# Turned signs in a seven-product step: the first weight sum becomes u0 + g0, added in place by an accumulating DMA, and the first feed-forward uses four such steps a pass instead of three

## The chip, the cores and the metric

The kernel runs on one core of a Trainium2 chip. The metric is the time of one execution on the device in microseconds, as the median of several runs. Before the change three runs gave 2245.61, 2246.25 and 2247.01 us.

## What is computed

One decoder layer on 256 tokens (T) of width 2048 (D), all in float32: a SwiGLU feed-forward (width 5632), a mixer of windowed attention and a recurrent part, an attention into a fixed memory, a second feed-forward, and a last norm. Only the two feed-forwards matter here:

```python
def swiglu(h, w_gate, w_up, w_down):
    return (jax.nn.silu(h @ w_gate) * (h @ w_up)) @ w_down

x = x + 0.5 * swiglu(rms_norm(x, ffn1_norm[l]), ffn1_w_gate[l], ffn1_w_up[l], ffn1_w_down[l])
# mixer, cross-attention
x = x + 0.5 * swiglu(rms_norm(x, ffn2_norm[l]), ffn2_w_gate[l], ffn2_w_up[l], ffn2_w_down[l])
```

## The kernel before, in words

**Two parts of each number.** A float32 value is kept as a high part `hi`, rounded to the type that TensorE multiplies fast, and a rest `lo`. ScalarE (ACT in the profile) makes `hi` by a cast (`split_unit`, L400), VectorE (DVE) makes `lo` by a subtraction (L401). One product of a 128-token block with a 128x512 block of weights is three matmuls of 512 columns, hi by hi, hi by lo and lo by hi (`times`, L474 to L479).

**Steps.** The feed-forward goes through column blocks of 512: `feed_forward` (L718) has a loop over groups of column blocks, and for each block j after the first one call of `gate_and_up`, which is one *pass* (ten a feed-forward). A pass multiplies the 256 tokens by the j-th 512 columns of the gate matrix and of the up matrix, over all 2048 rows. Its unit of work is a *step*, called q in the code, of 256 rows: two 128x512 blocks of gate, g0 and g1, and two of up, u0 and u1. A pass has eight steps, q = 0 to 7. `down` does the same for two column blocks of the down matrix. The order of the products is written in `product_pair` (L537).

**Seven products for eight.** With two blocks of tokens, two of rows and two matrices a step is a 2x2 by 2x2 block product: 8 products, 24 matmuls. In some steps a scheme of the Strassen kind takes 7 products (21 matmuls) and sums on both sides instead. The sums on the weight side are four 128x512 float32 operations on DVE (`divide`, L429 to L432); they fill two tiles t0 and t1, which are then split into `thi` and `tlo` like any weight (`two_parts`, L408 and L409). Of the tiles loaded, g0, g1 and u1 are still multiplied too, u0 is not. Which steps do so is listed by hand: `SEVEN = (0, 2, 4)` for the passes of the first feed-forward, `SEVEN_2 = (0, 2, 3, 4)` for those of the second, `SEVEN_DOWN` for the down matrix. Step 3 of the second feed-forward is *staged*: its sums are made during the mixer (`stage`, L371), written to a DRAM tensor `sums`, and read back by `load_sums` (L361). The sums on the token side are made once a feed-forward, in `combinations` (L489).

**Buffers and their order.** The SP queue loads the weights (`load`, L337): one DMA brings 1 MB, four blocks of one matrix, so that a gate tile and an up tile together feed two steps, (0,1), (2,3), (4,5) or (6,7). There are four such tiles, two pairs: the loads for the pair of steps after next start when DVE has read the last of a tile. `hi` and `lo` have three buffers each and are taken in turn, gate then up: the `hi` of a step's gate waits until TensorE has done with the up weights of two steps before, the `hi` of its up for the gate weights of the step before. `thi` and `tlo` have one buffer for each of t0 and t1. `next_item` (L436) divides one step ahead of TensorE. The program is written as one stream of instructions; a scheduler puts them in a fixed order on each engine before the run, and each engine then executes its own in that order, waiting on semaphores.

In the prediction, "behind" an instruction means after it in that fixed order.

Of the kernel before, what the change touches and what calls it, by code (L numbers as in the profile page):

```python
# [15 lines left out]
P = 128  # L16
# [120 lines left out]
def decoder_layer(ctx: ExitStack, tc: tile.TileContext, a: dict, out: bass.AP):  # L137
# [175 lines left out]
    for entry in weight_plan(a):  # L313
        if entry is None:
            ends.append(len(units))
            continue
        plan.append(entry)
        w, k0, nk, c0, n = entry
        if not isinstance(w, tuple):
            for k in range(k0, k0 + nk, KU):  # L320
                items.append(((len(units),), False))
                units.append((w, k, c0, n))
            continue
        for k in range(k0, k0 + nk, 2 * KU):
            u = len(units)
            units += [(v, k + i, c, 512) for v, c in zip(w, c0) for i in (0, KU)]
            for i in range(2):
                q = (k - k0) // KU + i
                if n == SEVEN_2 and q in STAGED:
# [3 lines left out]
    first_unused = {items[i][0][1] for i in staged}  # L333
    sums_d = dram.tile([len(staged), P, 4, 512], F32, name="sums")
    at = {"item": 0, "product": 0, "pool": None}

    def load(u, pieces=None):  # L337

        if u >= len(units) or u in raws:
            return  # L340
        w, k, c0, n = units[u]
        wide = at["pool"] is not None and (u < ends[0] or u >= ends[1] + LOADED)
        m = 2 if wide else 1
        if wide:
            raw = at["pool"].tile([P, m * KU, n], F32, tag="raw2", name="raw2", bufs=4)
# [4 lines left out]
        if u in first_unused:  # L350
            second = u + 1 in first_unused
            pieces = [(slice(1, 2), nc.sync)] + [(slice(2 + second, 4), nc.sync)]
            if not second:
                pieces = ((slice(1, 4), nc.sync),)
        elif u + 1 in first_unused and wide:
            pieces = ((slice(0, 2), nc.sync), (slice(3, 4), nc.sync))
        for i, queue in pieces or ((slice(0, m * KU), nc.sync),):
            rows = slice((k + i.start) * P, (k + i.stop) * P)
            queue.dma_start(raw[:, i], w[rows, c0 : c0 + n].rearrange("(a p) n -> p a n", p=P))

    def load_sums(i):  # L361

        if i not in staged or i in summed:
            return
        summed[i] = [
            wp.tile([P, KU, 512], F32, tag="raw", name="raw", bufs=4) for _ in range(2)
        ]
        for e, t in enumerate(summed[i]):
            nc.sync.dma_start(t[:], sums_d[staged[i], :, KU * e : KU * e + KU, :])

    def stage(t4, i, n):  # L371


        while at["item"] < STAGE_AT[n]:
            yield
        t = t4("su", (P, KU, 512)), t4("sg", (P, KU, 512))
        for e, v in zip(t, items[i][0][::-1]):
            w, k, c0, _ = units[v]
            rows = slice(k * P, (k + KU) * P)
            nc.sync.dma_start(e[:], w[rows, c0 : c0 + 512].rearrange("(a p) n -> p a n", p=P))  # L380
        yield from idle(4)
        u0, u1, g0, g1 = (e[:, c] for e in t for c in range(KU))
        with tc.issue_after(at["lo"].ins):
            dve.tensor_tensor(g0, u0, g0, ALU.subtract)
            dve.tensor_tensor(u0, u1, u0, ALU.subtract)
        yield
        with tc.issue_after(at["lo"].ins):
            dve.tensor_tensor(u1, u1, g0, ALU.subtract)
            dve.tensor_tensor(g1, g1, u1, ALU.subtract)
        yield from idle(8)  # L390
        for c, e in enumerate(t):
            nc.sync.dma_start(sums_d[n, :, KU * c : KU * c + KU, :], e[:])
# [8 lines left out]
            at["lo"] = dve.tensor_tensor(lo[:, s], raw[:, s], f32(hi[:, s]), ALU.subtract)  # L401
        return hi, lo

    def two_parts(v, e):
        sp = at["pool"]
        hi = sp.tile([P, KU, 512], F32R, tag="thi" + e, name="thi")
        lo = sp.tile([P, KU, 512], F32R, tag="tlo" + e, name="tlo")
        act.copy(hi[:], v[:])  # L408
        dve.tensor_tensor(lo[:], v[:], f32(hi[:]), ALU.subtract)  # L409
        return hi, lo  # L410

    def divide(i):


        if i >= len(items) or i in parts:
            return
        which, seven = items[i]
        if len(which) == 1:
            parts[i] = split_unit(*which)
            return  # L420
        g, u = which
        if not seven:
            parts[i] = split_unit(g), split_unit(u)
            return
        t = summed.get(i)
        if t is None:
            rg, ru = raws[g], raws[u]
            t = [wp.tile([P, KU, 512], F32, tag="raw", name="raw", bufs=4) for _ in range(2)]
            dve.tensor_tensor(t[1][:, 0], ru[:, 0], rg[:, 0], ALU.subtract)  # L429
            dve.tensor_tensor(t[0][:, 0], ru[:, 1], ru[:, 0], ALU.subtract)  # L430
            dve.tensor_tensor(t[0][:, 1], ru[:, 1], t[1][:, 0], ALU.subtract)  # L431
            dve.tensor_tensor(t[1][:, 1], rg[:, 1], t[0][:, 1], ALU.subtract)  # L432
# [56 lines left out]
    def combinations(sp, x: Act, seven, name, ready=lambda: True, early=True, n=0):  # L489
# [8 lines left out]
        def work():  # L498
# [3 lines left out]
            for q in pairs:  # L502
# [9 lines left out]
                    )  # L512
                if q in seven:
                    n = 4
                    dve.tensor_tensor(f[:, 0], v[:, 0, 1], v[:, 1, 1], ALU.add)
                    dve.tensor_tensor(f[:, 1], f[:, 0], v[:, 0, 0], ALU.subtract)
                    dve.tensor_tensor(f[:, 2], v[:, 0, 0], v[:, 0, 1], ALU.subtract)
# [19 lines left out]
    def product_pair(x: Act, c, w, first, middle, out):  # L537
# [67 lines left out]
    def gate_and_up(sp, x: Act, c, r, w):  # L605
# [5 lines left out]
            act.copy(hb[:, 0], b["p1"][:])  # L611

        def middle(b):
            dve.tensor_tensor(u2[:], b["p6"][:], hb[:, 0], ALU.add)
# [5 lines left out]
        def out(b, to):  # L620
            t = int(to in ("p4", "p5"))
            if to in ("p2", "p4"):
                dve.tensor_tensor(hb[:, t], b[to][:], u3[:] if t else hb[:, 0], ALU.add)
# [9 lines left out]
    def down(sp, h: Act, c, w, xs):  # L633

        u2, u3 = sums_of(sp)

        def half(x_, v):
            dve.scalar_tensor_tensor(x_, v, 0.5, x_, ALU.mult, ALU.add)

        def first(b):  # L640
            act.copy(u3[:], b["p1"][:])
# [1 line left out]
            half(xs[1][1], b["q"][:])  # L643

        def middle(b):
            dve.tensor_tensor(u2[:], b["p6"][:], u3[:], ALU.add)
            dve.tensor_tensor(u3[:], b["p7"][:], u2[:], ALU.add)
            dve.tensor_tensor(u2[:], b["p5"][:], u2[:], ALU.add)
            half(xs[1][0], u3[:])
            half(xs[1][1], u3[:])  # L650
            half(xs[0][1], u2[:])

# [65 lines left out]
    def feed_forward(sp, x, norm: Norm, wg, wu, wd, done, begin_last=lambda: None, last=False):  # L718
        if last:
            for tag, shape, dt, bufs in (  # L720
                ("hhi", [P, 16, T], F32R, 1), ("hlo", [P, 16, T], F32R, 1),
                ("hb", [P, 2, 512], F32, 2), ("thia", [P, KU, 512], F32R, 1),
                ("tloa", [P, KU, 512], F32R, 1), ("thib", [P, KU, 512], F32R, 1),
                ("tlob", [P, KU, 512], F32R, 1),
            ):
                sp.tile(shape, dt, tag=tag, name=tag, bufs=bufs)
        begun = at["item"]
# [966 lines left out]
```

## Time and profile before

| what | value |
|---|---|
| median of three runs | 2246.25 us |
| span of the profiled execution, first to last instruction | 2242.8 us |
| what lies around the span (median less span) | 3.45 us |
| TensorE (PE) busy | 2228.0 us, 99% |
| VectorE (DVE) busy | 1824.9 us, 81% |
| ScalarE (ACT) busy | 1248.6 us, 56% |
| GpSimd (POOL) busy | 129.8 us, 6% |
| HBM read, written | 436.30 MB, 23.59 MB |

The profile gives no time of its own for the profiled execution beside the span. PE is TensorE's matmul side, PEld its load of stationary data. A row of a group shows the line of the code, the engine, out<-in by tile names and sizes, how often, and the mean duration; one of the waits shows who waited for whom, in total, how often and the longest. In the timelines the first column is the start and the second the duration; consecutive matmuls overlap, so that their cost is the distance between starts. The tiles of the big weight loads go by the name `raw`, like the small ones.

### The profile page before, as it was taken

To read this page: it belongs to the slowest core of one execution; us is meant where nothing else is said; L and a number is where in the kernel's file an instruction comes from. 1 tells how busy PE (TensorE), PEld (TensorE's weight loads), DVE (VectorE), ACT (ScalarE), POOL (GpSimd) and SP (SyncE) were. 2 spreads that over 40 slices of the span, in tenths; PEclk is the share of its full clock that TensorE was granted. 3 is DMA by queue.
4 is the path that set the end of the run, shared out by engine and by line. 5 is a ranking of instruction groups with operands and counts; after the bars stand their busy time and mean duration, and the time that the engine had idled before them with its cause. 6 is when DMAs were issued, how large, how long until landed. Compare 5 with 4: busy or idle time off the path is not lost.

```text
span 2242.8 us, 28283 instructions
## 1 busy us (share of the span) xinstructions
PE 2228.0 (99%) x10587; PEld 1830.8 (82%) x10587; DVE 1824.9 (81%) x2365; ACT 1248.6 (56%) x1629; POOL 129.8 (6%) x197
## 2 busy tenths in 40 slices
PE   9999999999999999999999999999999999999998
PEld 7888888888888877788888888888888888888886
DVE  7898988998989476977657656547999999999997
ACT  6555555555556468544434546456565466555654
POOL 1000000000001001200321030001000000000000
PEclk9999999999999999999999999999999999999999
DMA  7555555555555544676668576547565566556564
GB/s 264 188 199 197 204 195 201 203 189 206 193 201 197 170 137 152 193 233 212 207 214 281 194 260 231 188 167 272 199 234 205 199 231 220 201 200 227 197 226 150
DMA packets 229705, 461.84 MB, mean 206 GB/s; under 512 B 15467, under 2 KB 17744, under 8 KB 229568
## 3 DMA queue, kind: packets, MB, share of 16 engines
q1 hardware_dynamic: 220512, 433.62, 56.7%
q0 software_dynamic: 8592, 25.62, 3.7%
q8 instruction: 83, 1.36, 0.2%
q10 hardware_dynamic: 464, 0.79, 0.1%
q14 instruction: 54, 0.44, 0.1%
HBM read 436.30 MB, written 23.59 MB: 205 GB/s over the span
## 4 chain that ended last, share of the span: by engine, by line
PE 97%; DVE 1%; DMA 1%; issue 1%; ACT 0%; SPq 0%; POOL 0%; POOLq 0%; DVEq 0%
PE acc L477 20%; PE acc L478 19%; PE acc L479 19%; PE mm L478 8%; PE mm L479 8%; PE mm L477 8%; PE tr L665 2%; PE tr L478 2%; PE tr L477 2%; PE tr L479 2%; PE mm L1349 1%; PE tr L1285 1%; DVE lo L401 0%; PE mm L912 0%; DMA raw<-in_ffn_w_gate_dram 0%
## 5 line engine op out<-in xcount | busy, mean ns | idle before, releaser
L400 ACT CAST hi<-raw 128x1024 fp32r<-128x1024 f32 (+1 forms) x770 | 756.2, 992 | 710.3 <-PE acc L479 509.5
L401 DVE TENSOR_TENSOR lo<-raw,hi 128x1024 fp32r<-128x1024 f32 (+1 forms) x770 | 882.4, 1149 | 307.7 <-ACT hi L400 306.0
L477 PE MATMUL acc<-hi,xhi 128*128 128x512 f32 (+1 forms) x1166 | 461.4, 396 | 2.5 <-ACT xhi L692 2.1
L478 PE MATMUL acc<-lo,xhi 128*128 128x512 f32 (+1 forms) x1166 | 452.9, 388 | 0.0
L479 PE MATMUL acc<-hi,xlo 128*128 128x512 f32 (+1 forms) x1166 | 452.4, 388 | 0.0
L477 PEld LDWEIGHTS acc<-hi,xhi 128*128 128x128 f32 x1166 | 219.3, 188 | 50.6 <-issue 4.0
L479 PEld LDWEIGHTS acc<-hi,xlo 128*128 128x128 f32 x1166 | 218.8, 188 | 45.7 <-DVE xlo L693 1.0
L478 PEld LDWEIGHTS acc<-lo,xhi 128*128 128x128 f32 x1166 | 219.2, 188 | 43.8 <-issue 1.7
L408 ACT CAST thi<-raw 128x1024 fp32r<-128x1024 f32 x192 | 199.7, 1051 | 62.2 <-DVE raw L431 41.8
L409 DVE TENSOR_TENSOR tlo<-raw,thi 128x1024 fp32r<-128x1024 f32 x192 | 232.3, 1219 | 1.2 <-ACT thi L408 0.4
L479 PE MATMUL acc<-hi,hlo 128*128 128x512 f32 x372 | 145.5, 391 | 0.0
L478 PE MATMUL acc<-lo,hhi 128*128 128x512 f32 x372 | 145.4, 391 | 0.0
L477 PE MATMUL mm<-hi,xhi 128*128 128x512 f32 x370 | 145.4, 393 | 0.0
L477 PE MATMUL acc<-hi,hhi 128*128 128x512 f32 x372 | 144.9, 390 | 0.0
L479 PE MATMUL mm<-hi,xlo 128*128 128x512 f32 x370 | 144.3, 390 | 0.0
L478 PE MATMUL mm<-lo,xhi 128*128 128x512 f32 x370 | 144.2, 390 | 0.0
L478 PEld LDWEIGHTS acc<-lo,hhi 128*128 128x128 f32 x372 | 69.9, 188 | 14.3
L477 PEld LDWEIGHTS acc<-hi,hhi 128*128 128x128 f32 x372 | 69.9, 188 | 14.3
L479 PEld LDWEIGHTS acc<-hi,hlo 128*128 128x128 f32 x372 | 69.9, 188 | 14.0
L479 PEld LDWEIGHTS mm<-hi,xlo 128*128 128x128 f32 x370 | 69.4, 188 | 14.5
L478 PEld LDWEIGHTS mm<-lo,xhi 128*128 128x128 f32 x370 | 69.5, 188 | 14.2
L477 PEld LDWEIGHTS mm<-hi,xhi 128*128 128x128 f32 x370 | 69.5, 188 | 14.1
(410 smaller groups left out, 3601.1 us busy)
## 6 DMA issues: line engine op xcount, KB each, us to landing
raw<-in_ffn_w_down_dram SPq DMA_DIRECT2D x88, 1024.0 KB, 5.2
raw<-in_ffn_w_gate_dram SPq DMA_DIRECT2D x84, 1024.0 KB, 5.1
raw<-in_ffn_w_up_dram SPq DMA_DIRECT2D x78, 1024.0 KB, 6.4
raw<-in_w_in_dram SPq DMA_DIRECT2D x136, 512.0 KB, 3.5
raw<-in_w_out_dram SPq DMA_DIRECT2D x32, 512.0 KB, 4.4
raw<-sums SPq DMA_DIRECT2D x20, 512.0 KB, 6.2
raw<-in_w_proj_attn_dram SPq DMA_DIRECT2D x16, 512.0 KB, 3.9
raw<-in_w_proj_rwkv_dram SPq DMA_DIRECT2D x16, 512.0 KB, 5.6
```

Source lines behind the costliest of these rows:

```text
L400: at["hi"] = act.copy(hi[:, s], raw[:, s])
L401: at["lo"] = dve.tensor_tensor(lo[:, s], raw[:, s], f32(hi[:, s]), ALU.subtract)
L408: act.copy(hi[:], v[:])
L409: dve.tensor_tensor(lo[:], v[:], f32(hi[:]), ALU.subtract)
L477: pe.matmul(o, xh, hi, start=first, stop=False, **how)
L478: pe.matmul(o, xh, lo, start=False, stop=False, **how)
L479: pe.matmul(o, xl, hi, start=False, stop=last, **how)
L665: pe.transpose(b[:, o : o + P], tok[:, t, col : col + P], ident[:])
L1285: pe.matmul(b[e][:, o : o + P], x1[r, j, cs_], x2[r, j, cs_], start=True, stop=True)
L1349: pe.matmul(vb[:, (o + k) * P : (o + k + 1) * P][:, r], lhs(k, e), rhs[:, k, r], start=first and k + e == 0, stop=True, **ek,)
```

## The change

Three things, all in the feed-forwards:

1. The signs of the seven-product scheme are turned, so that the first weight sum is u0 + g0 where it was u0 - g0. In `divide` DVE no longer makes this sum. Behind the load of an up tile, `load` issues one more DMA on the POOL queue, 256 KB with `accum_op=add`, which reads g0 from DRAM once more and adds it to u0 in place, for each step with seven products that isn't staged. The tile's first block then holds u0 + g0, and is split (`split_unit(u)` whole) and multiplied in its place, as the last of the seven products (p5), instead of as one half of t1. So t1 has one block in place of two.
2. For the staged step, row 0 of `sums` (u0 + g0) is loaded into the up tile where u0 would be, and `load_sums` loads the other three rows: two DMAs of 512 and 256 KB for two of 512 KB, and one of 256 KB more ahead of the up tile's load.
3. `SEVEN` becomes `(0, 2, 3, 4)`: in the ten passes of the first feed-forward step 3 has seven products too, and nothing staged.

The signs in `stage`, `combinations` and in the sums of the results follow. The core of the diff:

```diff
-SEVEN, SEVEN_DOWN = (0, 2, 4), ((2, 4, 6), (2, 4))
+SEVEN, SEVEN_DOWN = (0, 2, 3, 4), ((2, 4, 6), (2, 4))
...
+        first = [v for v in (u, u + 1)[:m] if v in first_sums]
+        for v in first:
+            nc.sync.dma_start(raws[v][:, 0], sums_d[first_sums[v], :, 0, :])
+        if first:
+            pieces = ((slice(1, 4), nc.sync),)
+            if first[0] > u:
+                pieces = ((slice(0, 2), nc.sync), (slice(3, 4), nc.sync))
...
+        for v in (u, u + 1)[:m]:
+            if v in added:
+                w, k, c0, n = units[added[v]]
+                pool.dma_start(
+                    raws[v][:, 0], w[k * P : k * P + P, c0 : c0 + n], accum_op=ALU.add,
+                )
...
-        for e, t in enumerate(summed[i]):
-            nc.sync.dma_start(t[:], sums_d[staged[i], :, KU * e : KU * e + KU, :])
+        for t, c, m in zip(summed[i], (1, 3), (2, 1)):
+            nc.sync.dma_start(t[:, :m], sums_d[staged[i], :, c : c + m, :])
...
-            dve.tensor_tensor(t[1][:, 0], ru[:, 0], rg[:, 0], ALU.subtract)
-            dve.tensor_tensor(t[0][:, 0], ru[:, 1], ru[:, 0], ALU.subtract)
-            dve.tensor_tensor(t[0][:, 1], ru[:, 1], t[1][:, 0], ALU.subtract)
-            dve.tensor_tensor(t[1][:, 1], rg[:, 1], t[0][:, 1], ALU.subtract)
-        a_ = two_parts(t[0], "a")
-        parts[i] = split_unit(g), split_unit(u, slice(1, 2)), (a_, two_parts(t[1], "b"))
+            dve.tensor_tensor(t[0][:, 0], ru[:, 1], ru[:, 0], ALU.add)
+            dve.tensor_tensor(t[0][:, 1], t[0][:, 0], rg[:, 0], ALU.subtract)
+            dve.tensor_tensor(t[1][:, 0], t[0][:, 0], rg[:, 1], ALU.add)
+        a_ = two_parts(t[0], "a", 2)
+        parts[i] = split_unit(g), split_unit(u), (a_, two_parts(t[1], "b", 1))
...
-                    ("p7", of_c(q, 2), of_w(ta, 0)), ("p6", of_c(q, 1), of_w(ta, 1)),
+                    ("p7", of_c(q, 2), of_w(ta, 1)), ("p6", of_c(q, 1), of_w(ta, 0)),
                     ("p1", of_x(0, k), of_w(g, 0)), ("p2", of_x(0, k + 1), of_w(g, 1)),
-                    ("p3", of_c(q, 3), of_w(u, 1)), ("p4", of_x(1, k + 1), of_w(tb, 1)),
-                    ("p5", of_c(q, 0), of_w(tb, 0)),
+                    ("p3", of_c(q, 3), of_w(u, 1)), ("p4", of_x(1, k + 1), of_w(tb, 0)),
+                    ("p5", of_c(q, 0), of_w(u, 0)),
```

In the changed kernel the first of the three sums, which reads the added tile, is L438, the others L439 and L440; the accumulating DMA is L366.

More of the change, by code (lines that the diff above doesn't have):

```diff
@@ L328, in decoder_layer @@
                 q = (k - k0) // KU + i
-                if n == SEVEN_2 and q in STAGED:
+                if len(ends) == 2 and n == SEVEN_2 and q in STAGED:
                     staged[len(items)] = len(staged)
@@ L332, in decoder_layer @@
     raws, parts, summed = {}, {}, {}
-    first_unused = {items[i][0][1] for i in staged}
+    first_sums = {items[i][0][1]: n for i, n in staged.items()}
+    added = {which[1]: which[0] for i, (which, seven) in enumerate(items) if seven and i not in staged}
     sums_d = dram.tile([len(staged), P, 4, 512], F32, name="sums")
@@ L349, in load @@
             raws[u + i] = raw[:, i * KU : (i + 1) * KU, :]
[L350 to L356, printed above, removed]
+        first = [v for v in (u, u + 1)[:m] if v in first_sums]
[5 more added lines that the diff above has]
+                pieces = ((slice(0, 2), nc.sync), (slice(3, 4), nc.sync))
+            elif len(first) == 2:
+                pieces = ((slice(1, 2), nc.sync), (slice(3, 4), nc.sync))
         for i, queue in pieces or ((slice(0, m * KU), nc.sync),):
@@ L383, in stage @@
         with tc.issue_after(at["lo"].ins):
-            dve.tensor_tensor(g0, u0, g0, ALU.subtract)
-            dve.tensor_tensor(u0, u1, u0, ALU.subtract)
+            dve.tensor_tensor(u0, u0, g0, ALU.add)
+            dve.tensor_tensor(u1, u1, u0, ALU.add)
         yield
         with tc.issue_after(at["lo"].ins):
-            dve.tensor_tensor(u1, u1, g0, ALU.subtract)
-            dve.tensor_tensor(g1, g1, u1, ALU.subtract)
+            dve.tensor_tensor(g0, u1, g0, ALU.subtract)
+            dve.tensor_tensor(g1, g1, u1, ALU.add)
         yield from idle(8)
@@ L402, in split_unit, with two_parts @@
         return hi, lo
-    def two_parts(v, e):
+    def two_parts(v, e, n):
         sp = at["pool"]
[L406 to L409, printed above, removed]
+        hi = sp.tile([P, n, 512], F32R, tag="thi" + e, name="thi")
+        lo = sp.tile([P, n, 512], F32R, tag="tlo" + e, name="tlo")
+        act.copy(hi[:], v[:, :n])
+        dve.tensor_tensor(lo[:], v[:, :n], f32(hi[:]), ALU.subtract)
         return hi, lo
@@ L613, in middle @@
         def middle(b):
[L614 removed]
+            dve.tensor_tensor(u2[:], b["p6"][:], hb[:, 0], ALU.subtract)
             dve.tensor_tensor(u3[:], b["p7"][:], u2[:], ALU.add)
@@ L622, in out @@
             if to in ("p2", "p4"):
-                dve.tensor_tensor(hb[:, t], b[to][:], u3[:] if t else hb[:, 0], ALU.add)
+                if t:
+                    dve.tensor_tensor(hb[:, 1], b[to][:], u3[:], ALU.subtract)
+                else:
+                    dve.tensor_tensor(hb[:, 0], b[to][:], hb[:, 0], ALU.add)
                 act.activation(hb[:, t], hb[:, t], AF.Silu, scale=r[t])
@@ L635, in down, with half @@
         u2, u3 = sums_of(sp)
-        def half(x_, v):
-            dve.scalar_tensor_tensor(x_, v, 0.5, x_, ALU.mult, ALU.add)
+        def half(x_, v, by=0.5):
+            dve.scalar_tensor_tensor(x_, v, by, x_, ALU.mult, ALU.add)
         def first(b):
@@ L645, in middle @@
         def middle(b):
-            dve.tensor_tensor(u2[:], b["p6"][:], u3[:], ALU.add)
+            dve.tensor_tensor(u2[:], b["p6"][:], u3[:], ALU.subtract)
             dve.tensor_tensor(u3[:], b["p7"][:], u2[:], ALU.add)
             dve.tensor_tensor(u2[:], b["p5"][:], u2[:], ALU.add)
-            half(xs[1][0], u3[:])
+            half(xs[1][0], u3[:], -0.5)
             half(xs[1][1], u3[:])
```

10 lines of the change are left out of this document (5 added, 5 removed).

## Prediction

> **What bounds the kernel now.** I read the page first (busy shares, the chain that ended last), then the busy time of two stretches, then TensorE's timeline over one pass, and the waits last.
>
> ```profile
> span 2242.8 us, 28283 instructions
> PE 2228.0 (99%) x10587; PEld 1830.8 (82%) x10587; DVE 1824.9 (81%) x2365; ACT 1248.6 (56%) x1629; POOL 129.8 (6%) x197
> ...
> PE 97%; DVE 1%; DMA 1%; issue 1%; ACT 0%; SPq 0%; POOL 0%; POOLq 0%; DVEq 0%
> ```
> ```profile
> 30.00:660.00 630.00, 630.00 (x2819) 519.80 (x2818) 571.80 (x718) 351.53 (x398) 7.86 (x15) 1.00 0.58 199
> 1510.00:2230.00 720.00, 720.00 (x3220) 590.76 (x3219) 657.89 (x827) 419.93 (x492) 8.69 (x13) 1.00 0.61 213
> ```
> ```profile
> 310.71 0.39 PE L477 MATMUL tr<-thi,chi 128*128 128x512 f32 x1
> ...
> 320.91 0.39 PE L477 MATMUL tr<-thi,chi 128*128 128x512 f32 x1
> ...
> 331.11 0.39 PE L477 MATMUL tr<-thi,chi 128*128 128x512 f32 x1
> ```
>
> The two stretches (columns: length, then busy time of PE, PEld, DVE, ACT and POOL, the granted clock, DMA share, GB/s) are the first and the second feed-forward. TensorE is busy in all of both, at full clock. The three PE rows are the first matmuls of steps 0, 2 and 4 of one pass: a step with seven products and one with eight, 21 + 24 = 45 matmuls, take 10.20 us, so one matmul costs 0.2267 us of TensorE, and nothing lies between. Whatever is saved elsewhere gains nothing; whatever comes late costs at once.
>
> How late may DVE be? Hardly:
>
> ```profile
> PEld tr L478 <- DVE tlo L409: 4.2, 13, 0.4
> ```
> ```profile
> DVE raw L429 <- DMA raw<-in_ffn_w_up_dram: 13.5, 13, 2.0
> ```
>
> Thirteen times PEld waits, for 0.4 us at most, for the `tlo` that a division made, and thirteen times the first weight sum (L429) waits for the load of up. So the chain load of up, sums, `thi`, `tlo`, TensorE has next to no slack in some steps, and the change lengthens just this chain.
>
> **The change part by part.**
>
> *Removed from TensorE.* Step 3 of ten passes goes from 24 to 21 matmuls: 30 x 0.2267 = **6.8 us**, all on the path.
>
> *DVE and ACT.* These rows have the durations:
>
> ```profile
> L401 DVE TENSOR_TENSOR lo<-raw,hi 128x1024 fp32r<-128x1024 f32 x662 | 809.1, 1223 | 293.6 <-ACT hi L400 291.9
> L409 DVE TENSOR_TENSOR tlo<-raw,thi 128x1024 fp32r<-128x1024 f32 x192 | 232.3, 1219 | 1.2 <-ACT thi L408 0.4
> L401 DVE TENSOR_TENSOR lo<-raw,hi 128x512 fp32r<-128x512 f32 x100 | 68.4, 685 | 7.7 <-ACT hi L400 7.7
> ...
> L429 DVE TENSOR_TENSOR raw<-raw,raw 128x512 f32<-128x512 f32 x86 | 59.0, 686 | 14.0 <-DMA raw<-in_ffn_w_up_dram 13.5
> ```
> ```profile
> L408 ACT CAST thi<-raw 128x1024 fp32r<-128x1024 f32 x192 | 199.7, 1051 | 62.2 <-DVE raw L431 41.8 <-DVE raw L432 8.1 <-PE tr L479 4.9
> ```
>
> A division with sums costs DVE 4 x 0.69 + 2 x 1.22 + 1.22 + 0.69 = 7.1 us before; after, 3 x 0.69 + 1.22 + 0.69 + 2 x 1.22 = 6.4 us, one sum less. A plain step costs 2 x 1.22 = 2.4, a staged one 4.35 before and after. In the first feed-forward ten steps go from 2.4 to 6.4 (+40) and 44 others save 0.7 (-30): DVE gains about 10 us of work in 630, from 91% to 93% of a stretch shortened to 623. That hides beside TensorE on average; if it didn't, those 10 us would come out once. The second feed-forward loses 42 x 0.7 = 29 us of DVE work, worth nothing by itself as PE is full there. ACT's casts have the same total columns a seven-product step; step 3 adds 1.7 us in ten passes to an engine at 56%. One more small float32 set in `combinations` runs once. The turned signs change no count.
>
> *Buffers.* The block u0 + g0 is now multiplied last (p5), where u1 was done two products earlier; so the `hi` of the gate two steps on waits 2 x 3 x 0.2267 = 1.4 us longer. In the listing of the instructions' order the scheduler has laid TensorE's work round this: in most passes it starts steps 2 to 4 with p1 and p2, which need no `thi`. I cost it at nothing; without that cover it is up to 1.4 us in 20 passes, 28 us.
>
> *Added to the chain: 96 accumulating DMAs on POOL* (40 + 14 in the first feed-forward, 30 + 12 in the second, with the down matrix). Each waits for the landing of its up load and then holds back L438. Behind it on POOL stand only other such DMAs, the four stores of x1d and the reloads of x3d, none due within 20 us. Behind L438 on DVE stand the same step's `lo` and sums, on ACT `thi`, then TensorE. No row of before has an accumulate. The nearest are POOL's loads:
>
> ```profile
> raw<-in_final_norm_dram POOLq DMA_DIRECT2D x4, 256.0 KB, 4.5
> ...
> g<-in_rwkv_g_dram POOLq DMA_DIRECT2D x4, 128.0 KB, 3.1
> ```
> ```profile
> x<-x1d POOLq DMA_DIRECT2D x4, 512.0 KB, 6.7
> ```
>
> The first has the same size, queue and stage of the kernel. I take d = **4.5 us** from the landing of up to that of the sum. Bounds: 3.1 (half the size) and 6.7 (twice the size, as the destination has to be read too).
>
> [...]
>
> *What covers d.* Step 4 is the tight one. Its up load and TensorE's first use of its sums, in the first and the last pass of the second feed-forward (the landing is the answer's last line, us after the issue):
>
> ```profile
> 1586.55 0.38 SPq L359 DMA_DIRECT2D raw<-in_ffn_w_up_dram  x1
> ```
> ```profile
> DMA to landing us min/median/max: 6.6/6.6/6.6
> ```
> ```profile
> 1600.75 0.61 PE L477 MATMUL tr<-thi,chi 128*128 128x512 f32 x2
> ```
> ```profile
> 2132.65 0.42 SPq L359 DMA_DIRECT2D raw<-in_ffn_w_up_dram  x1
> ```
> ```profile
> DMA to landing us min/median/max: 9.7/9.7/9.7
> ```
> ```profile
> 2147.50 0.49 PE L477 MATMUL tr<-thi,chi 128*128 128x512 f32 x1
> ```
>
> Up landed 7.6 and 5.1 us ahead of use; read the same way, the ten passes give 7.6, 6.7, 3.7, 8.0, 4.5, 6.0, 5.2, 7.3, 5.7, 5.1 (the sums tensor's loads share the queues there). In the first feed-forward I take 6.9: the load issued at 316.02 landed after 7.5 us, 7.6 ahead of the PE row at 331.11, less the 0.7 by which the new step 3 is shorter.
>
> ```profile
> 316.02 0.37 SPq L359 DMA_DIRECT2D raw<-in_ffn_w_up_dram  x1
> ```
> ```profile
> DMA to landing us min/median/max: 7.5/7.5/7.5
> ```
>
> From the start of L438 to the end of `thi` it takes three sums at a pitch of 0.60 us, one `lo` between them (1.14) and the cast (1.05): 4.0 us. The pitch is the distance of starts in these rows:
>
> ```profile
> 1681.24 1.22 DVE L409 TENSOR_TENSOR tlo<-raw,thi 128x1024 fp32r<-128x1024 f32 x1
> 1682.38 0.69 DVE L429 TENSOR_TENSOR raw<-raw,raw 128x512 f32<-128x512 f32 x1
> 1682.98 0.69 DVE L430 TENSOR_TENSOR raw<-raw 128x512 f32<-128x512 f32 x1
> 1683.58 0.69 DVE L431 TENSOR_TENSOR raw<-raw,raw 128x512 f32<-128x512 f32 x1
> ```
>
> In the listing one matmul stands ahead of the first `thi` in ten of the twenty passes (L438 must start 3.8 us before the step), and about nine in the other ten (1.9 us before; four of them in the second feed-forward, six in the first). The stall of a pass is d + 3.8 (or 1.9) less the lead:
>
> - second feed-forward, d = 4.5: 0.7, 1.6, 2.7, 0.3, 1.9, 2.3, 1.2, 1.0, 0.7, 3.2 = 15.6 us; DVE frees the tiles there up to 0.7 us earlier, which takes off 5.7: **9.9**;
> - first feed-forward: 4 x (4.5 + 3.8 - 6.9) = **5.6**, and nothing in the six others;
> - down: a few of 26 steps with leads of 7.6 to 7.9, 0.4 to 0.7 each: **2**;
> - steps 0, 2 and 3: leads over 9 us, or a second sum that DVE reaches 5 us later: nothing; at d over 5.2 they begin to count.
>
> Sum: 9.9 + 5.6 + 2 - 6.8 = **+10.7 us**: 2242.8 + 10.7 = 2253.5 of span, and with the 3.45 us around it **2257 us** against a median of 2246.25.
>
> *SP and traffic.* Ten more issues of 0.4 us on a queue that waits for tiles most of the time. 96 x 128 packets of 2 KB at about 92 ns, the mean of the first row below (0.567 x 16 x 2242.8 / 220512), are 71 us of one engine in sixteen, doubled for two reads: DMA share 58 to 61% goes up by 3 to 6 points. I take nothing for slower loads.
>
> ```profile
> q1 hardware_dynamic: 220512, 433.62, 56.7%
> ```
>
> **The rivals.**
>
> *Hidden: faster.* The accumulate lands within 2.8 us of up, or the leads grow as much, because loads and stalls space themselves out. Then only the matmuls count: -6.8 us, 2239.4; at d = 3.1 the same sum gives stalls of 4.7, so -2, 2244. For it: POOL is 6% busy, and just after up lands the next gate load isn't issued yet. Against it: 4.5 us for this size in this stage. It decides at d of 2.8 to 3, where the stalls are 2.5 to 4.
>
> *Heavy: much slower.* The accumulate costs like 512 KB, d = 6.7: stalls of 37.6 and 24.6 us, less 6.8, +55, 2302. For it: two reads, and two such DMAs beside the loads of steps 4 and 5 in the first feed-forward. Against it: a quiet moment in the queues.
>
> *The pair of edits cancels.* d of 3.1 to 4.0 gives -2 to +4. That the change doesn't do what it says is no case: the listing has 30 matmuls less and 96 accumulates.
>
> **How the numbers follow.** About 0.2% (4.5 us) is what a measurement of this kernel can tell from no change. Forecast, stalls outweigh the matmuls (2251 to 2284, d up to 5.9, which is the longest of the four 256 KB loads, 5.1, and 0.8 for a second read): 0.45. Hidden (2239 to 2242): 0.30. Cancels (within 0.2%): 0.17. Heavy (over 2284): 0.08. Faster 0.30, same 0.17, slower 0.53. Both signs hold much of the chance, so the forecast's own range is 2251 to 2284; the range for 8 in 10 reaches over the hidden case, 2239 to 2284.
>
> ```profile
> DMA to landing us min/median/max: 4.0/4.5/5.1
> ```
>
> **What would show it.** In the profile after: PE in 30:660 below 100% and waits of PEld or ACT `thi` on L438 to L440 at step 4; L438 waiting for a DMA on raw in more than 13 places, by d less the slack; L366's median to landing, which is d itself; 30 matmuls less on PE; DVE busy lower by some 19 us. If L366 lands in 3 us and no waits appear, the forecast is wrong and the hidden case right; if waits appear at steps 2 and 3 as much as at step 4, it is the buffers' order and not d. Loads of up that take longer than 6.4 us would mean that traffic, not the chain, is the price.
>
> ```profile
> raw<-in_ffn_w_up_dram SPq DMA_DIRECT2D x78, 1024.0 KB, 6.4
> ```

## The result, and the profile after

The changed kernel takes 2391.6 us against 2246.05 us of the kernel before (its median with a fourth run): 1.067 times as long, 95% interval 1.0645 to 1.0694. That is 146 us more, where 11 more were forecast and 38 more was the end of the range.

The page of the changed kernel, the same lines as of before:

```profile
span 2389.5 us, 28663 instructions
PE 2278.7 (95%) x10557; PEld 1839.0 (77%) x10557; DVE 1810.1 (76%) x2332; ACT 1260.0 (53%) x1649; POOL 213.7 (9%) x293
...
PE 48%; DMA 23%; DVE 22%; issue 5%; ACT 2%; SPq 0%; POOLq 0%; POOL 0%; DVEq 0%; ACTq 0%
```

Thirty matmuls are gone, as forecast, and DVE has 15 us less to do, where 19 were forecast. But the chain that ended last, once 97% PE, now runs for 23% through DMAs and for 22% through DVE. PE is busy for 50 us *more* although it has less to do, partly because some of its matmuls are slower, as is shown below. The two feed-forwards, in stretches of the same length (columns as in the prediction; the second begins 75 us later than before):

```profile
30.00:660.00 630.00, 588.03 (x2508) 467.18 (x2508) 524.03 (x654) 327.96 (x375) 48.24 (x62) 0.98 0.65 198
1585.00:2305.00 720.00, 675.55 (x2902) 542.00 (x2901) 577.42 (x712) 379.85 (x444) 41.67 (x51) 0.97 0.67 212
```

PE was busy in all of both; now it idles for 42 and 44 us there, at a granted clock of 0.98 and 0.97. The first feed-forward and its down matrix lost about 73 us and the second about 72, read from the starts of the stores `x1d` behind the first and `x3d` ahead of the second. The waits name the new instruction:

```profile
ACT thi L417 <- DVE raw L439: 126.2, 72, 5.7
...
DVE raw L438 <- DMA raw<-in_ffn_w_gate_dram: 112.1, 45, 6.6
...
PEld mm L486 <- DVE lo L410: 56.9, 26, 5.7
...
DVE raw L438 <- DMA raw<-in_ffn_w_down_dram: 41.1, 18, 5.6
PEld tr L485 <- ACT thi L417: 37.3, 28, 5.4
```

In 63 of 96 places DVE itself now stands still for the accumulate, 153 us in all (before: 13 places, 13.5 us, for the load). All accumulates (L366) together, and then, on the page, the loads of up and the accumulates on gate alone:

```profile
DMA to landing us min/median/max: 4.0/4.3/8.2
```
```profile
raw<-in_ffn_w_up_dram SPq DMA_DIRECT2D x78, 1024.0 KB, 7.0
raw<-in_ffn_w_gate_dram POOLq DMA_DIRECT2D x70, 256.0 KB, 4.3
```

The median is close to what was forecast; the mean is not: 5.0 us from issue to landing. From the landing of up it takes POOL another 0.6 us to issue, so that d is 5.7 us on average, and up to 8.7. One pass shows how a stall comes about. SP and POOL (start, duration, then what was issued), the landing of the POOL row, DVE, and PE:

```profile
354.90 0.37 SPq L362 DMA_DIRECT2D raw<-in_ffn_w_gate_dram  x1
356.00 0.37 SPq L362 DMA_DIRECT2D raw<-in_ffn_w_up_dram  x1
```
```profile
355.75 0.86 POOL L366 DMA_DIRECT2D raw<-in_ffn_w_gate_dram  x1 [12.86 <-DMA raw<-in_ffn_w_up_dram]
```
```profile
DMA to landing us min/median/max: 7.6/7.6/7.6
```
```profile
363.40 0.69 DVE L438 TENSOR_TENSOR raw<-raw 128x512 f32<-128x512 f32 x1 [5.70 <-DMA raw<-in_ffn_w_gate_dram]
364.01 1.22 DVE L410 TENSOR_TENSOR lo<-raw,hi 128x1024 fp32r<-128x1024 f32 x1
```
```profile
359.65 0.39 PE L485 MATMUL mm<-hi,xhi 128*128 128x512 f32 x1
365.29 0.80 PE L486 MATMUL mm<-lo,xhi 128*128 128x512 f32 x1 [5.25 <-DVE lo L410]
365.88 0.63 PE L487 MATMUL mm<-hi,xlo 128*128 128x512 f32 x1
366.31 0.63 PE L485 MATMUL acc<-hi,xhi 128*128 128x512 f32 x1
```

The accumulate of step 4 is issued between the two 1 MB loads that SP starts for the next steps, and takes 7.6 us instead of 4. L438 waits for it, `lo` of the gate stands behind L438, and PE stands still from 359.9 to 365.3. After that its matmuls start 0.43 us apart. The granted clock (last but two column) of the stretch behind the stall and of the next:

```profile
365.30:370.60 5.30, 5.30 (x13) 4.14 (x14) 5.30 (x7) 3.33 (x5) 0.00 (x0) 0.50 0.00 0
370.60:380.00 9.40, 9.40 (x46) 7.77 (x45) 6.52 (x8) 3.68 (x5) 0.00 (x0) 1.00 0.67 225
```

TensorE runs at half speed for 5.3 us. It does 13 matmuls there, and some 2.4 us are lost on top of the stall (5.3 less 13 x 0.2267), in time that counts as busy. The granted clock fell to 0.50 behind single stalls of 2.5 and 2.6 us, too.

From the distances between the starts of matmuls (beyond 0.2267 us each; distances of 0.40 to 0.46 us counted as half speed), each loss put to the L438 that ran last before it:

| step | L438 | mean d, us | stalls, us | half speed, us |
|---|---|---|---|---|
| step 0, both feed-forwards | 20 | 5.3 | 20.3 | 2.6 |
| step 2 | 20 | 4.8 | 9.7 | 1.2 |
| step 3, first | 10 | 7.3 | 4.1 | 0 |
| step 4, first | 10 | 6.1 | 28.0 | 6.8 |
| step 4, second | 10 | 7.2 | 35.1 | 9.6 |
| down | 26 | 5.3 | 20.6 | 6.8 |

These are 145 of the 153 us that have to be explained (146.7 of span and the 6.8 of matmuls saved); the rest is in pieces under 0.1 us and outside the feed-forwards. The table tells where the time was lost; the experiments show that this often isn't where it was caused.

### The profile page after: what moved, and what is told of

It is laid out like the page before. It is cut to its first block, busy times and chain, and to the rows that moved or that the text cites. A ratio compares the mean times of both kernels' runs of the same rounds, so it can differ in the third digit from the quotient of the medians.

```text
span 2389.5 us, 28663 instructions
## 1 busy us (share of the span) xinstructions
PE 2278.7 (95%) x10557; PEld 1839.0 (77%) x10557; DVE 1810.1 (76%) x2332; ACT 1260.0 (53%) x1649; POOL 213.7 (9%) x293
## 4 chain that ended last, share of the span: by engine, by line
PE 48%; DMA 23%; DVE 22%; issue 5%; ACT 2%; SPq 0%; POOLq 0%; POOL 0%; DVEq 0%; ACTq 0%
PE acc L485 11%; PE acc L486 11%; PE acc L487 11%; DVE lo L410 10%; DMA raw<-in_ffn_w_gate_dram 10%; DMA raw<-in_ffn_w_up_dram 7%; DMA raw<-in_ffn_w_down_dram 5%; DVE tlo L418 3%; PE mm L486 2%; PE mm L487 2%; PE mm L485 2%; PE tr L676 2%; DVE raw L439 2%; DVE raw L440 1%; ACT hi L409 1%
## 5 line engine op out<-in xcount | busy, mean ns | idle before, releaser
L409 ACT CAST hi<-raw 128x1024 fp32r<-128x1024 f32 (+1 forms) x770 | 801.6, 1045 | 786.4 <-PE acc L487 478.8
L410 DVE TENSOR_TENSOR lo<-raw,hi 128x1024 fp32r<-128x1024 f32 (+1 forms) x770 | 930.7, 1214 | 331.7 <-ACT hi L409 330.2
L485 PE MATMUL acc<-hi,xhi 128*128 128x512 f32 (+1 forms) x1136 | 450.6, 399 | 2.7 <-ACT xhi L703 2.3
L487 PE MATMUL acc<-hi,xlo 128*128 128x512 f32 (+1 forms) x1136 | 442.8, 390 | 0.0
L417 ACT CAST thi<-raw 128x1024 fp32r<-128x1024 f32 x212 | 168.3, 833 | 131.2 <-DVE raw L439 126.2
L418 DVE TENSOR_TENSOR tlo<-raw,thi 128x1024 fp32r<-128x1024 f32 x212 | 196.0, 950 | 2.2 <-ACT thi L417 1.9
L438 DVE TENSOR_TENSOR raw<-raw 128x512 f32<-128x512 f32 x96 | 66.1, 689 | 153.3 <-DMA raw<-in_ffn_w_gate_dram 112.1
L366 POOL DMA_DIRECT2D raw<-in_ffn_w_gate_dram x70 | 60.4, 904 | 882.2 <-DMA raw<-in_ffn_w_up_dram 342.4
L486 PE MATMUL mm<-lo,chi 128*128 128x512 f32 x200 | 80.5, 402 | 5.6 <-DVE lo L410 5.6
L485 PE MATMUL mm<-hi,chi 128*128 128x512 f32 x200 | 80.7, 413 | 3.4 <-DVE u L638 1.8
```

The costliest lines, as they stand in the source:

```text
L366: pool.dma_start(raws[v][:, 0], w[k * P : k * P + P, c0 : c0 + n], accum_op=ALU.add,)
L409: at["hi"] = act.copy(hi[:, s], raw[:, s])
L417: act.copy(hi[:], v[:, :n])
L418: dve.tensor_tensor(lo[:], v[:, :n], f32(hi[:]), ALU.subtract)
L438: dve.tensor_tensor(t[0][:, 0], ru[:, 1], ru[:, 0], ALU.add)
L485: pe.matmul(o, xh, hi, start=first, stop=False, **how)
```

## The experiments

All kernels are edits of the changed kernel, e3, e11, e12 and e14 of its version e1; ratios are to the kernel before, run on the same chip, with 95% intervals. The kernel before took 2244.7 to 2246.05 us in these sets of runs, so differences of 1 us or so between the kernels below mean nothing. "Losses" are stalls and half speed counted as above, but with the pieces under 0.1 us, in stretches that hold one feed-forward; before they are 8 and 9 us, after 82 and 80.

**What is it: the accumulate, or the rest?**

e1: no accumulate, the same sum on DVE.

```diff
-            if v in added:
+            if False and v in added:
...
+            dve.tensor_tensor(ru[:, 0], ru[:, 0], rg[:, 0], ALU.add)
             dve.tensor_tensor(t[0][:, 0], ru[:, 1], ru[:, 0], ALU.add)
```

> Turned signs and four pairs kept, no accumulating DMA: VectorE makes u0 + g0 in place (96 sums of 0.69 us more on it). Theory chain (what costs is the wait for the accumulate, 4.9 us in the median, in the fixed orders of VectorE and ScalarE): the stalls go, 30 matmuls less count, VectorE is near full in the first feed-forward: 2240 to 2256 us. Rival scheme (turned signs, u multiplied last and the buffers' order, or the fourth pair itself cost): stays above 2300 us.

Measured: 2255.6 us, 1.0051 (1.0036 to 1.0066). Nearly all of the 146 us hangs on the accumulate. What remains is lost in the first feed-forward:

```profile
30.00:660.00 630.00, 624.85 (x2759) 504.91 (x2758) 604.77 (x769) 360.99 (x413) 7.89 (x15) 1.00 0.57 196
```

DVE is busy for 96% of it and PE idles for 5 us, so the 6.8 us of matmuls don't come out there.

e12: e1 with three pairs, so the turned signs alone.

```diff
-SEVEN, SEVEN_DOWN = (0, 2, 3, 4), ((2, 4, 6), (2, 4))
+SEVEN, SEVEN_DOWN = (0, 2, 4), ((2, 4, 6), (2, 4))
```

> Turned signs with all sums on VectorE and the first feed-forward with three pairs: no accumulate, no fourth pair. It parts the 10 us by which the kernel with the sum on VectorE is behind the kernel before. If the fourth pair costs (VectorE near full in the first feed-forward, 7 us net): 2244 to 2250 us. If the signs and the buffers' order cost: 2252 to 2262 us.

Measured: 2248.5 us, 1.0012 (1.0003 to 1.0022). The signs, and u0 + g0 held until the last product, cost some 3 us (1 to 5 by the interval); with all sums on DVE the fourth pair costs 7 us net.

e2: the same edit of `SEVEN` in the changed kernel, so the accumulate with three pairs.

> The accumulate and the turned signs kept, the first feed-forward back to three pairs (step 3 with eight products, 86 accumulates). Theory chain: step 3's own stalls (4.1 us) go and step 4 keeps most of its own; 6.8 us of matmuls come back: 2365 to 2400 us, the second feed-forward unchanged within 2 us. Rival fourth pair: most of what the first feed-forward lost (about 73 us) comes back, 2330 us or less.

Measured: 2400.2 us, 1.0695 (1.0668 to 1.0721). This is the upper end of what the first theory gave. With ten accumulates less and no second one behind step 2's, nothing is won. The fourth pair isn't the cause.

**Traffic, order, size?**

e3: e1, and beside it the same DMAs into a tile that nothing reads.

```diff
...
+                pool.tensor_copy(side[:, :1], raws[v][:, 1, :1])
                 pool.dma_start(
-                    raws[v][:, 0], w[k * P : k * P + P, c0 : c0 + n], accum_op=ALU.add,
+                    side[:], w[k * P : k * P + P, c0 : c0 + n], accum_op=ALU.add,
                 )
...
```

> As the kernel with the sum on VectorE, and an accumulating DMA of the same size from the same source and at about the same moment into a side tile that nothing waits for: the traffic without the wait. Theory chain: within 10 us of that kernel, under 2265 us; loads of up take 0.6 us longer as in the changed kernel, and it doesn't matter. Rival traffic (the loads made longer by it are the cost): over 2300 us, stalls at loads and not at sums.

Measured: 2284.6 us, 1.0176 (1.0159 to 1.0193). 29 us more than e1, between the two forecasts: my "it doesn't matter" was wrong, and yet the traffic is a fifth of the whole. In it loads of up take 7.2 us in the median (6.8 in e1, which has no accumulate), and DVE's first sum waits for them for 31 us (9 in e1):

```profile
L444 DVE TENSOR_TENSOR raw<-raw,raw 128x512 f32<-128x512 f32 x96 | 65.5, 685 | 30.9 <-DMA raw<-in_ffn_w_up_dram 28.7 <-DMA raw<-in_ffn_w_down_dram 2.1
```

The one-column copy on POOL that ties the DMA to the landing of up also held tiles for 26 us in three places, so 29 us is rather too much.

e4: the gate's split written ahead of the sums.

```diff
+        g_ = split_unit(g)
         t = summed.get(i)
...
-        parts[i] = split_unit(g), split_unit(u), (a_, two_parts(t[1], "b", 1))
+        parts[i] = g_, split_unit(u), (a_, two_parts(t[1], "b", 1))
```

> The changed kernel with the gate's split written ahead of the sums, so that the lo of the gate stands ahead of the first sum in VectorE's order and no longer behind it. Theory order (the cover p1 and p2 was itself queued behind the waiting sum): the stalls before mm<-lo,xhi (34 us) and some of the half-speed time go: 2335 to 2370 us. Rival latency alone: the same wait is met a few matmuls later at thi, within 12 us of 2391.

Measured: 2403.0 us, 1.0704 (1.0662 to 1.0746). TensorE's waits for `lo` ahead of an `mm` fell from 46.4 to 14.1 us, and came back ahead of `thi` (26.6 us there became 45.3) and elsewhere. That `lo` stands behind L438 decides only which matmul is the first to wait. This theory fell.

e6: half of the columns; the kernel leaves out half of the sum u0 + g0.

```diff
-                    raws[v][:, 0], w[k * P : k * P + P, c0 : c0 + n], accum_op=ALU.add,
+                    raws[v][:, 0, : n // 2], w[k * P : k * P + P, c0 : c0 + n // 2], accum_op=ALU.add,
```

> The accumulates take 256 of the 512 columns, 128 KB in place of 256 (half of the sum u0 + g0 is left out). Theory fixed latency (d in a quiet moment is issue and round trip, not bytes): the median from issue to landing goes from 4.3 to 3.7 to 4.2 us, the time to 2345 to 2385 us, mostly by less traffic. Rival bytes: median under 3 us, time under 2330 us.

Measured: 2351.2 us, 1.0463 (1.0434 to 1.0492); from issue to landing:

```profile
DMA to landing us min/median/max: 2.9/3.2/7.7
```

The median fell by 1.1 us, more than I gave it and less than the rival did, and 40 us came back. The longest, 7.7 us, is nearly as long as with all columns (8.2): that isn't size.

**Whose stall is it?**

e7 and e8: accumulates everywhere but at step 4, and only there; elsewhere the sum is made on DVE.

```diff
     added = {
         which[1]: which[0] for i, (which, seven) in enumerate(items)
-        if seven and i not in staged
+        if seven and i not in staged and rows_of[i] != (4, False)
     }
...
+            if u not in added:
+                dve.tensor_tensor(ru[:, 0], ru[:, 0], rg[:, 0], ALU.add)
```

`rows_of` holds the number of each step and whether it is one of the down matrix. In e8 the condition is `rows_of[i] == (4, False)`.

> Accumulates everywhere but in step 4 of the twenty passes, where VectorE makes the sum (76 accumulates stay). Theory step (each accumulate costs the stall that stands at its own step; 63 us of stalls and 16 of half-speed matmuls stood at step 4): 2391.6 - 80 = 2305 to 2325 us. Rival loop (a late sum makes the tile free late and so the next loads, and stalls are shared over a pass): less than 2300, as the other steps' stalls shrink too, or above 2340, as the lateness shows at another step.

> The reverse: accumulates only in step 4 of the twenty passes (20 stay), the others on VectorE. Theory step: 2255.6 of the kernel with no accumulate, and 70 to 80 of step 4's stalls: 2320 to 2340 us. Rival loop: under 2300 us, as step 4 meets loads that come earlier when the steps ahead of it aren't late.

Measured: e7 2339.2 us, 1.0413 (1.0382 to 1.0444); e8 2291.9 us, 1.0208 (1.0192 to 1.0225). e7 lies between its two forecasts, e8 is the loop's. Step 4 showed 79 us of losses; without its accumulates 52 come back, and by themselves they cost 36 over e1. The losses of e8 in the first feed-forward are 21 us, as in e1: the ten accumulates at step 4, where the changed kernel showed 35 us, cost nothing there when they are alone. So what stands at step 4 of the first feed-forward came with the accumulates of the steps ahead. In the second, e8's losses are 48 us against 12. From issue to landing, e8 in the first and in the second feed-forward:

```profile
DMA to landing us min/median/max: 3.9/4.0/4.2
```
```profile
DMA to landing us min/median/max: 4.8/6.4/7.0
```

One DMA, of one size, at one step, takes 4.0 us in the one and 6.4 in the other. What differs is when SP issues its next loads. An accumulate of the first feed-forward and one of the second, each with SP's loads:

```profile
324.64 0.87 POOL L371 DMA_DIRECT2D raw<-in_ffn_w_gate_dram  x1 [41.99 <-DVE tlo L423]
```
```profile
327.27 0.37 SPq L367 DMA_DIRECT2D raw<-in_ffn_w_gate_dram  x1
```
```profile
1871.07 0.85 POOL L371 DMA_DIRECT2D raw<-in_ffn_w_gate_dram  x1 [44.79 <-DVE lo L415]
```
```profile
1871.05 0.38 SPq L367 DMA_DIRECT2D raw<-in_ffn_w_gate_dram  x1
1873.41 0.38 SPq L367 DMA_DIRECT2D raw<-in_ffn_w_up_dram  x1
```

In the ten passes of the first feed-forward SP issues its next load 0.9 to 2.8 us behind the accumulate, in those of the second from 2.1 us ahead of it to 0.2 us behind. The loads of the staged sums have landed by then, or do so within 1.3 us. The 4.0 us are hidden, the 6.4 are paid for.

**Where does the lateness come from?**

e5: the block that is added to is loaded first, by a DMA of its own.

```diff
+        cuts = [0] + [KU * i + 1 for i in range(m) if u + i in added] + [KU * i for i in range(1, m) if u + i in added]
+        if len(cuts) > 1 and not pieces:
+            cuts = sorted(cuts) + [m * KU]
+            pieces = [(slice(s, e), nc.sync) for s, e in zip(cuts, cuts[1:])]
```

> The changed kernel with the load of an up tile cut, so that the block that is added to lands by a DMA of its own (256 KB), ahead of the rest, and the accumulate can start beside the rest of the load. Theory latency (what stalls is landing plus d, one behind the other): the sum lands some 2 to 3 us earlier: 2290 to 2345 us. Rival loop (the tile's whole turnaround, its loads and traffic are the limit, so the rest of the tile is as late as before): over 2370 us.

Measured: 2357.0 us, 1.0491 (1.0473 to 1.0508): 35 us come back, between the forecasts.

e11: e1, with no wait for a DMA ahead of any sum, but behind the last read of a tile a 256 KB load overwrites one of its blocks, for which the tile's next load has to wait.

```diff
+        if wide and (u in added or u + 1 in added):
+            held[u + 1] = w[k * P : k * P + P, c0 : c0 + n]
...
+    def keep_tile(u):
+        if u in held:
+            pool.dma_start(raws[u][:, 1], held[u])
...
+        keep_tile(u)
```

> The kernel with the sum on VectorE, and no wait for any DMA in the sums; but behind the last read of each up tile that had an accumulate (86 tiles) a 256 KB load overwrites one block of it, and only when that has landed may the tile's next load start. It adds about 4.3 us to the tile's turnaround and nothing to the chain from load to sums. Theory turnaround: as dear as the wait for the accumulate, 2330 us or more. Rival chain (the wait ahead of the sum itself is the cost): traffic only, 2265 to 2290 us.

Measured: 2319.1 us, 1.0327 (1.0311 to 1.0342), 63 us over e1; SP now waits in 84 places for these loads:

```profile
SPq L364 <- DMA raw<-in_ffn_w_up_dram: 373.0, 60, 9.0
SPq L364 <- DMA raw<-in_ffn_w_down_dram: 148.3, 24, 7.5
```

A delay that adds nothing to the chain from load to sums costs 63 us, about twice what traffic alone does in e3. The 63 hold the traffic of these loads too; what that is worth by itself wasn't tried, and by e3's 29 us the late release alone would be some 34. So a tile's turnaround has next to no slack: what makes it free late makes its next load late. It isn't the 75 or more that the theory put on it, and it is more than the rival's 10 to 35. The rest fits a wait ahead of the sum that costs by itself, as e8's 36 us do; this is argued, not shown.

e9 and e10: five tiles in place of four in e9, four in its control e10; to make room, step 6 of the down matrix has eight products in both.

```diff
-SEVEN, SEVEN_DOWN = (0, 2, 3, 4), ((2, 4, 6), (2, 4))
+SEVEN, SEVEN_DOWN = (0, 2, 3, 4), ((2, 4), (2, 4))
...
-            raw = at["pool"].tile([P, m * KU, n], F32, tag="raw2", name="raw2", bufs=4)
+            raw = at["pool"].tile([P, m * KU, n], F32, tag="raw2", name="raw2", bufs=5)
```

> The changed kernel with five tiles of 1 MB for the loads in place of four. To make room, step 6 of the down matrix has eight products (8 steps, 24 matmuls or 5.4 us more, 8 accumulates less), as in the next run, which has four tiles. Theory turnaround (a tile lives for its load, the accumulate and the division of its two steps, 23 to 25 us, where four tiles allow 20.5; the lateness of every accumulate goes on to the next load, and shows at step 4): nearly all stalls go, 2250 to 2290 us. Rival traffic and queues (the loads and the accumulate collide, however many tiles): above 2350 us.

> The control for the run with five tiles: the changed kernel with four tiles and step 6 of the down matrix with eight products. 5.4 us of matmuls more and 8 accumulates less, by 1.1 to 1.4 us each: both theories 2384 to 2400 us.

Measured: e9 2330.6 us, 1.0374 (1.0358 to 1.0389); e10 2413.2 us, 1.0745 (1.0728 to 1.0763), 13 us above the forecast for the control. One tile more brings back 83 us; e9 lies between its two forecasts, so that turnaround isn't the whole either. The first feed-forward, five tiles and then four:

```profile
30.00:660.00 630.00, 614.21 (x2694) 497.03 (x2693) 553.31 (x680) 351.48 (x397) 49.60 (x63) 0.99 0.70 212
```
```profile
30.00:660.00 630.00, 575.67 (x2420) 459.39 (x2419) 494.49 (x610) 311.80 (x354) 45.25 (x58) 0.96 0.62 189
```

The matmuls in the same 630 us go from 2420 to 2694. Losses there fall from 105 to 35 us, in the second only from 88 to 71.

e14 and e15: the floor of that arrangement (five tiles, all sums on DVE), and five tiles without the ten accumulates at step 4 of the second feed-forward. e14 has the edits of e9 in e1; e15 has in e9 the selection of e7, for the second feed-forward only:

```diff
+        if seven and i not in staged and not (rows_of[i] == (4, False) and n_of[i])
```

> Five tiles and no accumulate, the sum on VectorE: the floor of that arrangement. 2255.6 of the four-tile kernel with the sum on VectorE and 5.4 us for 24 matmuls more: 2250 to 2265 us. If five tiles by themselves cost (order of the loads, queue): above 2275 us.

> Five tiles, accumulates everywhere but in step 4 of the ten passes of the second feed-forward, where VectorE makes the sum (82 stay). Theory chain at step 4 (its own accumulate, issued beside the loads of the staged sums, lands too late, and that is 45 us of what is left): 2280 to 2298 us. Rival lateness handed on from step 0 and 2: above 2315 us.

Measured: e14 2248.7 us, 1.0014 (1.0005 to 1.0024), losses 15 and 9 us; e15 2280.0 us, 1.0147 (1.0131 to 1.0164), losses 36 and 27. Ten accumulates, those at step 4 of the second feed-forward, are 50 us with five tiles, and not handed on from steps 0 and 2. And with five tiles the four pairs fit beside DVE: e14 has 24 matmuls (5.4 us) more than e1 and takes 7 us less, a little less than forecast. So some 12 of the 83 us that the fifth tile brought back come without any accumulate.

e13: e9 and e5 together.

> Five tiles, and the block that is added to loaded by a DMA of its own ahead of the rest of its tile. Theory (two costs: the tile's turnaround, which five tiles relieve, and in the second feed-forward the chain from load to sum at step 4, which the early block shortens by some 2 us): 2285 to 2315 us against 2330.6. Rival (with five tiles the rest is traffic, collisions of the transfers): 2325 us or more.

Measured: 2443.9 us, 1.0878 (1.0859 to 1.0897), the slowest of all. The theory gave 2285 to 2315; the rival, collisions of the transfers, gave 2325 or more, and it holds. The accumulates now start while the 1 MB load that SP issues next is under way, nearly all of them:

```profile
DMA to landing us min/median/max: 4.1/6.7/9.0
```

The early start is lost again in a DMA of 6.7 us (4.3 in e9). That this collision is the whole reason is read from the trace; no run tries it by itself.

No version beat the kernel before. e12 comes nearest, without accumulate and fourth pair, and of those with the fourth pair e14: without its 5.4 us of down matmuls it would be some 2 us below by this sum, but no run has five tiles beside the whole scheme.

## Why the prediction was wrong

The direction was right, and so was the wait (L438 waits for the accumulate, and TensorE has no slack). The size was not, 146 us for 11: the time d was mis-sized where it counts, and the leads that were to cover it were taken as fixed. By the steps of the prediction:

- **Removed from TensorE, 6.8 us; DVE's 10 us hide beside it.** The first holds, 30 matmuls are gone. The second wasn't tried as it was forecast: with all sums on DVE, and DVE at 96% of the stretch for the 93% of the forecast, the fourth pair costs 7 us net (e1 less e12). With the accumulate it brings no gain clear of noise (2391.6 us with it, 2400.2 without, e2; the single runs overlap).
- **Buffers, nothing.** Holds within some 3 us (e12).
- **d = 4.5 us from the landing of up.** The size was off, and so was taking one number. Three groups can be told apart among the 96. For 22 of them SP had a load under way that it had issued ahead of the accumulate, or issued one at most 0.3 us behind it: these took 6.5 us on average from issue to landing. The ten at step 3, issued right behind those of step 2 on the same queue, took 6.1. The other 64 took 4.3. With POOL's issue 0.6 us after the landing, d is 4.8 at step 2, 6.1 and 7.2 at the two steps 4, and 7.3 at step 3, whose sum DVE reaches later. I had the 6.7 row and called it the heavy case, at 0.08, "a quiet moment in the queues" speaking against it. That reason was wrong at step 4, above all in the second feed-forward, where all ten belong to the 22: when up has landed, DVE has just let go of a tile, and SP has issued the next load. The first rival's quick accumulate never came, as none of the 96 took less than 4.0. The 0.8 us that the range allowed for a second read stand in no row, and no run shows such a read by itself; the quickest accumulate took 1.1 us more than the quickest plain load of its size (4.0 us, and 2.9 in e11), and in the packet records of the changed kernel's trace the packets of 2 KB of the accumulates took 214 ns on average, those of the SP queue 98.
- **How the loads delay it.** In the same records, the first packet of an accumulate moved 1.6 us after its issue on average in the 64, and 3.8 us after it in the 22; from there both groups took 2.7 to 2.8 us to land. In the stall shown above both moved side by side then: 32 packets of the accumulate and 32 of SP's loads start between 361.0 and 361.5 us. But nearly all of the delay stands ahead of the accumulate's first packet, and why that one moves so late no run here shows.
- **What covers d.** This is the step that failed most. I took the leads of before as fixed and charged each step with its own stall. Where only step 4 has an accumulate this comes out about right: in e8 d is 6.8 us on average in the second feed-forward, where my sum gives 33 to 39 us for that (with the 5.7 taken off or not), and e8 costs 36 over e1. With accumulates at every step it doesn't: even with d = 6.7 everywhere it gave +55, not +146. A tile's next load can't start before DVE has read the tile, four tiles leave that loop next to no slack, and a late sum makes a load late. Steps 0, 2 and 3 and down, where I had 2 us, show 65 in the table. e8 shows it from one side (step 4 of the first feed-forward alone costs nothing), e11 from another (late release costs 63, its traffic included), e9 from the third (one more tile gives 83 back, some 12 of them without any accumulate).
- **Covers p1 and p2.** They did start without `thi`, but their `lo` stood behind L438. e4 shows that this is no price of its own.
- **SP and traffic, nothing.** It was up to 29 us (e3). My sign for it misled: loads of up went from 6.4 to 7.0 us, but e1, with no accumulate, has 6.8 already.
- **Not in the sum at all:** half speed behind the stalls, 27 us, read from the granted clock.

A sum that follows the experiments: signs 3, fourth pair 7, traffic up to 29, and the remainder, 107 or more, for waiting for the accumulates. The half-speed matmuls, 27 us, are inside these. What stays open is how the 107 part between the wait ahead of the sums and the tiles' turnaround: late release and wait feed each other, and the experiments don't add up to separate shares (52 less without step 4, 36 more with it alone).

## What to carry to other kernels

Before moving a sum from a busy engine to a DMA, follow the tile round its whole loop: if the buffer's next load waits for that tile, the DMA's time can be paid at every round (a late release cost 63 us in e11, its traffic included), and leads read from the old trace are no safe cover, because a late load shrinks them (step 4 of the first feed-forward lost 35 us behind the accumulates of the steps ahead, and in e8, without them, nothing over e1). Take a DMA's duration from the moment in which it will run, and look which transfers are issued just ahead of it (the accumulate of step 4 took 4.0 us in the first feed-forward of e8 and 6.4 in the second, in the median); the release that starts it can be the release that starts its competitors. And where a full TensorE is made to wait in many small pieces, look at the granted clock: behind the stalls here it cost 27 us that the waits don't list.

## What the runs showed of the hardware

- An accumulating DMA of 256 KB from HBM into SBUF on POOL took 4.0 us from issue to landing at the least (3.9 in e5), one of 128 KB 2.9 (e6): from these two, an estimate of 1.1 us for 128 KB on top of some 1.8. A plain load of 256 KB on the same queue took 2.9 at the least, the minimum of the loads that hold the tiles in e11:

```profile
DMA to landing us min/median/max: 2.9/4.4/7.4
```

- With a load of the SP queue issued ahead of it and still under way, or issued at most 0.3 us behind it, the same accumulate took 4.2 to 8.2 us, 6.5 on average (22 of the changed kernel), and up to 9.0 in e13. Two accumulates issued right behind each other, 0.5 to 0.9 us apart, took 4.2 and 6.1 us on average (ten pairs).
- In the changed kernel, stalls of 2.3 to 5.4 us were followed by a granted clock of 0.5, at which 512 columns took 0.43 us and not 0.2267, for some 2.6 to 5.5 us of matmuls (the record of the granted clock has 0.5 for 3.4 or 6.8 us each time in the feed-forwards). Not every one was: the clock stayed at 1.0 behind one of 3.3 us, and behind one of 2.9 shortly after a smaller one.
